# A tiny tanh in the first stage, and the last tile's convolution input ahead of its latents (two-layer decoder trunk, one core)

## The chip, the cores and the metric

The kernel runs on one core of a Trainium2 chip. The metric is device time of one execution in microseconds. Three runs of the kernel before took 896.16, 896.84 and 897.67 us; the median, 896.84 us, is the time before.

The core's engines work in parallel, each through its own instructions in a fixed order: TensorE (PE in the profile, with its weight loads as PEld), VectorE (DVE), ScalarE (ACT), GpSimd (POOL), and SyncE (SP), whose queue starts the DMAs. Semaphores hold an instruction until what it needs from another engine is done; all that stands behind it on its engine waits too.

## The reference

```python
D_MODEL, SEQ, DEPTH = 1024, 256, 2
for l in range(DEPTH):
    mod = c_act @ w_mod[l] + b_mod[l]                       # adaLN
    sh1, sc1, g1, sh2, sc2, g2 = jnp.split(mod, 6, axis=-1)
    h = modulate(rms_norm(x, mix_norm_g[l]), sh1, sc1)
    # token_mixer(h):
    z = h @ w_in
    q_lat, kv_lat, k_rope, qkv_b, conv_in, gate_logits = split(z)
    ...                                                     # o_a: MLA attention from q_lat, kv_lat, k_rope
    ...                                                     # o_b: MoBA attention from qkv_b
    glu_a, glu_g = jnp.split(conv_in, 2, axis=-1)
    u = glu_a * jax.nn.sigmoid(glu_g)
    u = causal_depthwise_conv(u, conv_dw_w, conv_dw_b)      # 31 taps
    o_c = silu(layer_norm(u)) @ w_conv_pw2 + b_conv_pw2
    y = (g[0] * o_a + g[1] * o_b + g[2] * o_c) @ w_out      # g: sigmoid gates
    x = x + g1 * y
    h = modulate(rms_norm(x, ffn_norm_g[l]), sh2, sc2)
    x = x + g2 * channel_mixer(h)                           # w_up, 3-tap conv, silu(a) * b, w_down
```

All inputs are fp32. x is 256 tokens by 1024 channels.

## The kernel before

Channels lie on the 128 partitions, tokens along the row, so x is 8 tiles (k = 0 to 7) of 128 x 256. Every fp32 product is made of three matmuls: each operand is split into a high part (`hi`, rounded by ACT's copy, L234) and a low part (`lo`, DVE's difference, L235), and PE adds hi*hi, hi*lo and lo*hi in one PSUM bank (L324, L325, L327). So each weight unit that SP loads (L206, tile `raw`) passes ACT (`whi`), then DVE (`wlo`), and then PE. `raw`, `whi` and `wlo` have four buffers each: a load waits until DVE has read the unit four before it, a split until PE is through with that unit's parts.

`all_units` lists the weight units in the order in which they are loaded and split; `take` hands them out in that order and keeps loads ahead (`AHEAD0`, two in the first stage). The program is written in one order, and the tile framework places each engine's instructions from it with priorities, so rows of different steps are interleaved. `issue_after` pins an instruction behind another.

The first stage of layer 0 is the loop `for k in range(KD)` in `layer`. For each tile k:

- ACT makes `e`, the modulated tile (L920), and from it `hh` (L921); DVE makes `hl` (L922). Both are operands for all of the layer's input projections.
- `latents(k)` adds the tile's part of q_lat, kv_lat and k_rope to three `psb` banks (weights 128x672), `conv_in(k)` that of the convolution input to four `psa` banks (128x1024).
- `prepare_tile(k + 1)` makes the next tile's modulation on DVE: one row of w_mod times c (1024 wide, L834) for tiles 0 to 3, two for 4 to 7, then `mod`, `mq` and `gs` (L836, L845, L841), on which the next `e` waits.
- After tile 2, ACT makes the sines for the rotary tables, with a function table of their own (L512).

Behind the loop the order of STEPS[0] begins: GLU0 to GLU3 (`glu`, L987 tanh on ACT, L988 product on DVE, which frees a psa bank each), LE0 and LE1 (`lat_evac`, the latents go from PSUM to SBUF on ACT, L955 to L958), LR0 (`lat_rstd`, three squares with sums on ACT, L967, `rs` on DVE, L544, and a power on POOL, L545), QKV00 (first of four units of the MoBA queries, into two psa banks), LR1, LT (`lat_T`: PE transposes the latents into psb banks, L975, two matmuls each, five pairs; ACT makes `qlh`/`klt` of them, L977, DVE `qll`/`klt`, L978), and QKV01 to QKV03. `kr` (L1136 to L1138) is the rotary key, which needs POOL's power. The 31 taps of the convolution (`cacc`, L1167 and L1170) are spread over the mixer on DVE. psa has five banks, of which the convolution input holds four; psb has three.

The tanh of the GLU and the sines are in different function tables, so ACT_TABLE_LOAD stands ahead of the first sine and, before the change, ahead of the first tanh of the GLU (L987).

Of the kernel before, what the change touches and what calls it, by code (L numbers as in the profile page):

```python
# [13 lines left out]
AF = mybir.ActivationFunctionType  # L14
# [7 lines left out]
KD = 8  # L22
# [36 lines left out]
LEAD = 16  # L59

LEADS = {(0, "G", 1, 0): 0, (0, "G", 1, 1): 40, (1, "G", 3, 0): 0, (1, "G", 3, 1): 40,
         (1, "in", 1): 0, (1, "in", 2): 40, (0, "up", 4, 0): 0, (0, "up", 4, 1): 40, (0, "up", 8, 0): 0, (0, "up", 8, 1): 40,
         (1, "up", 2, 1): 0, (1, "up", 3, 1): 40, (1, "up", 8, 0): 0, (1, "up", 8, 1): 40}
# [97 lines left out]
def trunk_kernel(ctx, tc, xT, crow, ccol, pos, invf, modb_d, cols_d, grow_d, wmh, wmr, wm, win1, wqkv,  # L161
                  wgc, wgab, wuq, wukv, woab, woc, wout, wup, wdn, out):
    nc = tc.nc
    te, ac, ve, gp, sy = nc.tensor, nc.scalar, nc.vector, nc.gpsimd, nc.sync
# [8 lines left out]
    def nm(s):  # L173
        uid[0] += 1
        return f"{s}_{uid[0]}"
# [4 lines left out]
    def psb():  # L180
        return psp.tile([P, 512], F32, tag="psb", name=nm("psb"), bufs=3)

    def e1():
        return wk.tile([P, S], F32, tag="e1", name=nm("e1"), bufs=8)
# [14 lines left out]
    def small(n, tag="sm", bufs=12):  # L199
        return wk.tile([P, n], F32, tag=tag, name=nm(tag), bufs=bufs)  # L200
# [37 lines left out]
    def chop(src, n, c, size=1024):  # L238

        m = max(1, size // c)  # L240
        return [(src[:, k0 * c:min(n, k0 + m) * c], range(k0, min(n, k0 + m))) for k0 in range(0, n, m)]

    def token_units(l, t):

        if t[0] == "KL":
            return [(win1[l, t[1], :, 0:672], [0])]
        if t[0] == "QKV":
            return [chop(wqkv[l, t[1], t[2] // 2], 4, 512)[t[2] % 2]]
        if t[0] in ("UQ", "UK"):
            return chop(wuq[l], 3, 768) if t[0] == "UQ" else chop(wukv[l], 2, 1024)  # L250
        if t[0] in ("C", "G"):
            return [chop((wgc if t[0] == "C" else wgab)[l, t[1]], KD, S)[t[2]]]
        if t[0] == "O":
            return chop(woab[l, t[1]], 1, 1024)
        if t[0] == "OC" and t[1] % 2 == 0:
            return chop(woc[l, t[1] // 2], 1, 1024)
        if t[0] == "PR" and t[1] % 2 == 0:
            return chop(wout[l, t[1] // 2], 2, 1024)
        return []

    def all_units():
        for l in range(L):
            for k in range(KD):
                if l == 0:
                    yield win1[l, k, :, 0:672], [0], LEAD
                yield win1[l, k, :, 672:1696], [0], LEADS.get((l, "in", k), LEAD)
            for t in CFG["order"][l]:
                yield from ((*u, LEADS.get((l, *t), LEAD)) for u in token_units(l, t))
            if l == 1:
                for first in (0, NRAW):  # L270
                    for i in range(2):
                        for j in range(first, first + NRAW):
                            yield *chop(wup[l, j], KD, S)[i], LEADS.get((l, "up", j, i), LEAD)
            for up, j in FFN[l]:
                if up and l == 1 and j < 2 * NRAW:
                    continue
                for i, u in enumerate(chop(wup[l, j], KD, S) if up else chop(wdn[l, j], 1, 1024)):
                    yield *u, LEADS.get((l, "up", j, i), LEAD) if up else LEAD

    ahead, later = [AHEAD0], [0]  # L280
    coming, raws_in, ready = list(all_units())[::-1], [], []

    def split_rest(keep=0):
# [16 lines left out]
    def take1():  # L300
        return take()[0][0][1]
# [10 lines left out]
    def flush(whole=False):  # L312
        if whole:

            banks = list(dict.fromkeys(id(o.tensor) for o, *_ in queue))
            queue.sort(key=lambda q: banks.index(id(q[0].tensor)))
            for o, p1, p2, p3, start, stop in queue:
                te.matmul(o, p1[0], p1[1], start=start, stop=False)
                te.matmul(o, p2[0], p2[1], start=False, stop=False)
                newest[0] = te.matmul(o, p3[0], p3[1], start=False, stop=stop)  # L320
            queue.clear()
            return newest[0]
        for o, p1, p2, _, start, _ in queue:
            te.matmul(o, p1[0], p1[1], start=start, stop=False)  # L324
            te.matmul(o, p2[0], p2[1], start=False, stop=False)  # L325
        for o, _, _, p3, _, stop in queue:
            last = te.matmul(o, p3[0], p3[1], start=False, stop=stop)  # L327
        queue.clear()
        return last

    def cut(w, i, n):
        return w[0][:, i * n:(i + 1) * n], w[1][:, i * n:(i + 1) * n]
# [23 lines left out]
    ones = cst.tile([P, 1], F32, name="ones")  # L356
# [62 lines left out]
    def mod_row(row, l, r, k, tag=None, scale=1.0):  # L419

        return use_row(wload_row(l, r, k, tag), row, l, r, k, scale)
# [57 lines left out]
    def step(gen, n=1):  # L479
        for _ in range(n):  # L480
            next(gen, None)
# [315 lines left out]
    def layer(l):  # L797
# [55 lines left out]
        def rows(pp, w, k, b, start, stop):  # L853
            mmv(pp, (hh[:, k, b * P:(b + 1) * P], hl[:, k, b * P:(b + 1) * P]), w, start, stop)

        def cols2(pp, w, k, first, last):
            for i in range(2):
                mmw(pp[:, i * S:(i + 1) * S], cut(w, i, P), (hh[:, k, :], hl[:, k, :]), first and i == 0,
                    last and i == 1)
# [15 lines left out]
        def gate_c(u, part, last=1, bank=psb):  # L875
            pp = pair(("C", u), part, bank)
            if part == last:
                if not gated:
                    gated.append(wk.tile([P, KD, S], F32, tag="thc", name=nm("thc"), bufs=1, align_bytes=LINE))
                ac.activation(gated[0][:, 2 * u:2 * u + 2, :].rearrange("p c t -> p (c t)"), pp, AF.Tanh, scale=0.5)  # L880
# [5 lines left out]
        def latents(k):  # L886
            if k == 0:
                plat.extend(psb() for _ in range(3))
            w = take1()
            st, sp = (k == 0), (k == KD - 1)  # L890
            for b in range(NB):
                rows(plat[b][:, 0:416], [v[:, 0:416] for v in w], k, b, st, sp)
                rows(plat[2][:, b * S:(b + 1) * S], [v[:, 416:672] for v in w], k, b, st and b == 0, sp and b == 1)
            flush()

        def conv_in(k):
            w = take1()
            for j in range(4):
                cols2(pci[j], cut(w, j, S), k, k == 0, k == KD - 1)
            flush()  # L900

        def tile(k):
            tiles.append(norm_tile(k, bc, gs1[:, k:k + 1], sh1[:, k:k + 1], hh, hl))
# [6 lines left out]
        for k in range(KD):  # L910
            if l > 0:
                if k + 3 < KD:
                    tile(k + 3)
                hold[0] = [i.ins for i in tiles[-1]]
                conv_in(k)
                hold[0] = None
                mod_row(crow1[0], l, 2, k, scale=0.5 if CDMA else 1.0)
                continue
            t = e1()
            ac.activation(t, xn[k // 4][:, k % 4, :], AF.Identity, scale=gains[k], bias=sh1[:, k:k + 1])  # L920
            at = ac.activation(hh[:, k, :], t, AF.Copy)  # L921
            last = ve.tensor_tensor(hl[:, k, :], t, hh[:, k, :].bitcast(F32), op=ALU.subtract)  # L922
            if HOLD > 1:
                hold[0] = [last.ins]
            with tc.issue_after(wlast[0].ins) if k == 0 else ExitStack():
                latents(k)
            if k == 2:
                with tc.issue_after(at.ins):
                    step(trigs)
            if k + 1 < KD:  # L930
                prepare_tile(k + 1)
            conv_in(k)
            if k in C0K:
                gate_c(0, C0K[k], 3, psa)
            hold[0] = None
# [576 lines left out]
    for l in range(L):  # L1512
        layer(l)
# [86 lines left out]
```

## Time and profile before

| | before |
|---|---|
| median of 3 runs | 896.84 us |
| profiled execution | 897.64 us |
| its span | 895.5 us |
| granted TensorE clock | 0.999 |
| DMA, mean over the span | 225 GB/s |
| first instruction of tile 6 on PE | 50.21 us |
| GLU's first tanh on ACT | 61.13 us |

The span runs from the first to the last instruction of the profiled execution; 2.14 us lie around it. In the timeline a row has start, duration, engine, line, operation, output<-inputs with shapes, a count where equal neighbours are merged, and in brackets the idle time just before it with what ended it. "By starts" means from the start of one instruction to the start of the next on its engine: since work is pipelined, that is a little shorter than its duration. Lines L are those of the kernel before; in the changed kernel they stand 1 lower in the file up to the stage's loop (L234 and L235 are unchanged) and 7 lower behind it.

### The profile page before, as it was taken

To read this page: it belongs to the slowest core of one execution; us is meant where nothing else is said; L and a number is where in the kernel's file an instruction comes from. 1 tells how busy PE (TensorE), PEld (TensorE's weight loads), DVE (VectorE), ACT (ScalarE), POOL (GpSimd) and SP (SyncE) were. 2 spreads that over 40 slices of the span, in tenths; PEclk is the share of its full clock that TensorE was granted. 3 is DMA by queue.
4 is the path that set the end of the run, shared out by engine and by line. 5 is a ranking of instruction groups with operands and counts; after the bars stand their busy time and mean duration, and the time that the engine had idled before them with its cause. 6 is when DMAs were issued, how large, how long until landed. Compare 5 with 4: busy or idle time off the path is not lost.

```text
span 895.5 us, 18568 instructions
## 1 busy us (share of the span) xinstructions
PE 876.3 (98%) x7233; PEld 833.4 (93%) x7233; DVE 806.8 (90%) x1592; ACT 555.6 (62%) x998; POOL 47.0 (5%) x36
## 2 busy tenths in 40 slices
PE   7899999999999999999999999999999999999998
PEld 6888888999998999999989988989999899999998
DVE  6989999999988989999956999999987899999774
ACT  4677588734756655455635676887575676646551
POOL 1000700000000000000000043000000000000000
PEclk9999999999999999999999999999999999999999
DMA  8956634689998788988725565156866475887631
GB/s 320 369 207 200 206 116 159 205 290 329 308 334 290 248 281 283 329 302 281 257 95 156 187 215 185 48 180 208 298 208 210 147 234 160 284 304 234 194 97 48
DMA packets 57975, 201.58 MB, mean 225 GB/s; under 512 B 6944, under 2 KB 8480, under 8 KB 57888
## 3 DMA queue, kind: packets, MB, share of 16 engines
q1 hardware_dynamic: 57888, 200.41, 67.0%
q8 instruction: 56, 0.92, 0.4%
q14 instruction: 31, 0.25, 0.1%
HBM read 199.33 MB, written 1.05 MB: 224 GB/s over the span
## 4 chain that ended last, share of the span: by engine, by line
PE 78%; DVE 12%; DMA 4%; ACT 4%; issue 2%; SPq 0%; DVEq 0%; ACTq 0%
PE psb L324 16%; PE psb L325 16%; PE psb L327 15%; PE psa L327 8%; PE psa L324 8%; PE psa L325 7%; DVE wlo L235 3%; DVE cacc L1170 2%; ACT whi L234 2%; DVE raw L834 1%; DMA raw<-in_wup 1%; PE psa L432 1%; PE psa L752 1%; PE psa L764 1%; DMA raw<-in_win 1%
## 5 line engine op out<-in xcount | busy, mean ns | idle before, releaser
L234 ACT ACTIVATE whi<-raw 128x1024 fp32r<-128x1024 f32 (+2 forms) x286 | 295.2, 1041 | 162.2 <-PE psb L325 79.1
L235 DVE TENSOR_TENSOR wlo<-raw,whi 128x1024 fp32r<-128x1024 f32 (+2 forms) x286 | 339.2, 1192 | 37.7 <-ACT whi L234 30.1
L324 PE MATMUL psb<-hh,whi 128*128 128x256 f32 x1056 | 254.6, 282 | 0.9 <-ACT hh L633 0.5
L325 PE MATMUL psb<-hl,whi 128*128 128x256 f32 x1056 | 252.3, 279 | 0.0
L324 PEld LDWEIGHTS psb<-hh,whi 128*128 128x128 f32 x1056 | 198.6, 188 | 5.5 <-issue 3.0
L325 PEld LDWEIGHTS psb<-hl,whi 128*128 128x128 f32 x1056 | 198.7, 188 | 0.1
L327 PE MATMUL psb<-hh,wlo 128*128 128x256 f32 x1056 | 144.5, 278 | 0.0
L327 PEld LDWEIGHTS psb<-hh,wlo 128*128 128x128 f32 x1056 | 131.3, 188 | 0.4 <-issue 0.3
L1170 DVE SCALAR_TENSOR_TENSOR cacc<-upad,cw,cacc 128x256 f32<-128x256 f32 x240 | 105.5, 475 | 0.5
L324 PE MATMUL psa<-mhl,whi 128*128 128x256 f32 x400 | 93.2, 276 | 0.0
L325 PE MATMUL psa<-mhl,whi 128*128 128x256 f32 x400 | 93.1, 277 | 0.0
L545 POOL TENSOR_TENSOR rs<-rs,mhalf 128x8 f32<-128x8 f32 (+3 forms) x26 | 45.5, 1763 | 671.7 <-DVE rs L544 671.6
L325 PEld LDWEIGHTS psa<-mhl,whi 128*128 128x128 f32 x400 | 74.9, 188 | 0.0
L324 PEld LDWEIGHTS psa<-mhl,whi 128*128 128x128 f32 x400 | 74.9, 188 | 0.0
L1468 DVE SCALAR_TENSOR_TENSOR e<-psb,fw,e 128x255 f32<-128x255 f32 (+1 forms) x168 | 69.7, 472 | 3.6 <-ACT e L1464 3.6
L415 DVE SCALAR_TENSOR_TENSOR raw<-raw,crow 128x1024 f32<-128x1024 f32 x56 | 67.9, 1214 | 0.0
L327 PE MATMUL psa<-mhl,wlo 128*128 128x256 f32 x400 | 53.5, 276 | 0.0
L327 PEld LDWEIGHTS psa<-mhl,wlo 128*128 128x128 f32 x400 | 49.1, 188 | 0.0
L1464 ACT ACTIVATE e<-psb,fb,fw 128x256 f32<-128x256 f32 x84 | 42.2, 553 | 4.4 <-PE psb L327 4.4
L1472 ACT ACTIVATE e<-e 128x256 f32<-128x256 f32 x44 | 18.2, 414 | 40.6 <-DVE e L1468 40.6
L1476 ACT ACTIVATE mhl<-e 128x256 fp32r<-128x256 f32 x44 | 18.2, 413 | 40.1 <-DVE e L1474 40.1
L324 PE MATMUL psb<-whi,hh 128*128 128x416 f32 (+1 forms) x96 | 31.0, 351 | 5.2 <-ACT hh L921 5.2
(295 smaller groups left out, 1525.5 us busy)
## 6 DMA issues: line engine op xcount, KB each, us to landing
raw<-in_wup SPq DMA_DIRECT2D x88, 512.0 KB, 5.2
raw<-in_wmr SPq DMA_DIRECT2D x68, 512.0 KB, 5.6
raw<-in_wdn SPq DMA_DIRECT2D x44, 512.0 KB, 4.5
raw<-in_wgab SPq DMA_DIRECT2D x32, 512.0 KB, 4.8
raw<-in_wqkv SPq DMA_DIRECT2D x24, 512.0 KB, 4.8
raw<-in_wm SPq DMA_DIRECT2D x24, 512.0 KB, 4.8
raw<-in_win SPq DMA_DIRECT2D x16, 512.0 KB, 5.3
raw<-in_wgc SPq DMA_DIRECT2D x16, 512.0 KB, 4.3
```

The source lines that it names most:

```text
L234: ac.activation(hi, raw, AF.Copy)
L235: ve.tensor_tensor(lo, raw, hi.bitcast(F32), op=ALU.subtract)
L324: te.matmul(o, p1[0], p1[1], start=start, stop=False)
L325: te.matmul(o, p2[0], p2[1], start=False, stop=False)
L327: last = te.matmul(o, p3[0], p3[1], start=False, stop=stop)
L415: ve.scalar_tensor_tensor(raw, raw, scale, row, op0=ALU.mult, op1=ALU.mult, accum_out=acc)
L545: gp.tensor_tensor(r, r, mhalf[:, :n], op=ALU.pow)
L1170: ve.scalar_tensor_tensor(aj, upad[:, j, t:t + S], cw[:, j * 31 + t:j * 31 + t + 1], aj, op0=ALU.mult, op1=ALU.add)
L1464: ac.activation(t, src, AF.Identity, scale=fw[:, 2, c:c + 1], bias=fb[:, c:c + 1])
L1468: ve.scalar_tensor_tensor(t[:, d:S], src[:, 0:S - d], fw[:, 2 - d, c:c + 1], t[:, d:S], op0=ALU.mult, op1=ALU.add)
L1472: ac.activation(th, ab[0], AF.Tanh, scale=0.5)
L1476: ac.activation(mh, th, AF.Copy)
```

## The change

```diff
     def all_units():
         for l in range(L):
             for k in range(KD):
+                two = [(win1[l, k, :, 672:1696], [0], LEADS.get((l, "in", k), LEAD))]
                 if l == 0:
-                    yield win1[l, k, :, 0:672], [0], LEAD
-                yield win1[l, k, :, 672:1696], [0], LEADS.get((l, "in", k), LEAD)
+                    two.insert(0 if k < KD - 1 else 1, (win1[l, k, :, 0:672], [0], LEAD))
+                yield from two
...
             with tc.issue_after(wlast[0].ins) if k == 0 else ExitStack():
-                latents(k)
+                if k < KD - 1:
+                    latents(k)
             if k == 2:
                 with tc.issue_after(at.ins):
                     step(trigs)
+            if k == 4:
+                with tc.issue_after(at.ins):
+                    ac.activation(small(1, "m0", 4), ones, AF.Tanh)
             if k + 1 < KD:
                 prepare_tile(k + 1)
             conv_in(k)
+            if k == KD - 1:
+                latents(k)
```

In layer 0, a tanh of one column is placed behind `hh` of tile 4, and its table load with it. In tile 7 the 1024-wide unit of the convolution input is loaded, split and used ahead of the 672-wide unit of the latents. The instructions of the two kernels are otherwise the same; their order changes in more places, since the framework places them anew.

**ACT at the end of the first stage.** Before, from `hh` of tile 6 (`whi_674` is tile 7's 672-wide unit, `whi_703` its 1024-wide one, `whi_737` that of QKV00):

```order
L234 ACTIVATE whi_674<-raw_672 128x672
L921 ACTIVATE hh_135<-e_110_668 128x256
L234 ACTIVATE whi_703<-raw_701 128x1024
L920 ACTIVATE e_121_731<-mq_257,mod_100,gs_698 128x256
L921 ACTIVATE hh_135<-e_121_731 128x256
L234 ACTIVATE whi_737<-raw_735 128x1024
L234 ACTIVATE whi_755<-raw_753 128x1024
L955 ACTIVATE ma_831<-psb_293 128x384
```

Now (`whi_676` is tile 7's 1024-wide unit, `whi_705` its 672-wide one, `whi_739` QKV00, `whi_769` QKV01, `whi_855` QKV02):

```order
L922 ACTIVATE hh_135<-e_111_670 128x256
L234 ACTIVATE whi_676<-raw_674 128x1024
L234 ACTIVATE whi_705<-raw_703 128x672
L921 ACTIVATE e_122_733<-mq_257,mod_100,gs_700 128x256
L234 ACTIVATE whi_739<-raw_737 128x1024
L922 ACTIVATE hh_135<-e_122_733 128x256
L234 ACTIVATE whi_769<-raw_767 128x1024
L234 ACTIVATE whi_855<-raw_853 128x1024
L994 ACTIVATE e_143_821<-psa_285 128x256
```

QKV00's split moved between `e` and `hh` of tile 7, QKV02's split moved ahead of the GLU, and the GLU's tanh (L994) ahead of the latents' evacuation, with no table load before it.

**PE between tiles 6 and 7**, now (before, tile 7's latents stood here directly behind tile 6):

```order
L328 MATMUL psa_288<-hh_135,wlo_643 128x256 x2
L325 MATMUL psa_851<-whi_739,hh_135 128x512
L326 MATMUL psa_851<-whi_739,hl_136 128x512
L325 MATMUL psa_285<-hh_135,whi_676 128x256
L325 MATMUL psa_286<-hh_135,whi_676 128x256
```

The first two matmuls of QKV00 (`psa_851`, the fifth bank) moved ahead of all of tile 7.

**DVE behind the GLU's products.** Before (`wlo_854` and `wlo_860` are QKV02 and QKV03, `rs_846` the sums of the first 128 tokens, `kr_834` their rotary key, `qll` the latents' low parts):

```order
L235 TENSOR_TENSOR wlo_854<-raw_851,whi_853 128x1024
L544 TENSOR_SCALAR rs_846<-lss_841 128x3
L235 TENSOR_TENSOR wlo_860<-raw_857,whi_859 128x1024
L978 SCALAR_TENSOR_TENSOR qll_810<-psb_883,col_146,qlh_809 128x256
L978 SCALAR_TENSOR_TENSOR qll_810<-psb_888,col_146,qlh_809 128x256
L544 TENSOR_SCALAR rs_880<-lss_875 128x3
L1136 TENSOR_SCALAR kr_834<-kr_834,rs_846 128x32
```

Now:

```order
L235 TENSOR_TENSOR wlo_862<-raw_859,whi_861 128x1024
L545 TENSOR_SCALAR rs_848<-lss_843 128x3
L1177 SCALAR_TENSOR_TENSOR cacc_1299<-upad_814,cw_803,cacc_1299 128x256
L1143 TENSOR_SCALAR kr_836<-kr_836,rs_848 128x32
L985 SCALAR_TENSOR_TENSOR qll_812<-psb_885,col_146,qlh_811 128x256
L545 TENSOR_SCALAR rs_882<-lss_877 128x3
L1144 TENSOR_TENSOR kr_836<-kr_836,ta_793 128x32
L985 SCALAR_TENSOR_TENSOR qll_812<-psb_890,col_146,qlh_811 128x256
```

`kr`, which waits for POOL's power of `rs_848`, moved ahead of the first `qll`, and a tap stands between `rs_848` and it.

**PE at the fourth pair of transposes.** Before, they stood inside QKV01 (`whi_755`); now they follow its last matmul:

```order
L328 MATMUL psa_852<-wlo_770,hh_135 128x512
L982 MATMUL psb_900<-ident,ma_833 128x128
L982 MATMUL psb_900<-ident,ma_838 128x128
L325 MATMUL psa_851<-whi_855,hh_135 128x512
L982 MATMUL psb_905<-ident,ma_833 128x128
```

`psb_900` takes the bank of the first pair, so it waits until `qll` of `psb_885` has read that, and `psb_905` until `qll` of `psb_890` has. On SP the two loads of tile 7's input weights trade places (the 1024-wide one now comes first); on POOL nothing moves.

## The prediction

> **What bounds the kernel now.** I read the page's busy shares first, then the stretches, then TensorE's waits behind the first stage, and last the timeline between 38 and 70 us, engine by engine.
>
> ```profile
> PE 876.3 (98%) x7233; PEld 833.4 (93%) x7233; DVE 806.8 (90%) x1592; ACT 555.6 (62%) x998; POOL 47.0 (5%) x36
> ...
> 40.00:62.00 22.00, 19.63 (x144) 18.36 (x142) 19.39 (x48) 13.44 (x26) 0.00 (x0) 1.00 0.75 281
> 62.00:112.00 50.00, 49.84 (x249) 42.13 (x249) 49.69 (x106) 35.02 (x59) 19.22 (x9) 1.00 0.59 191
> ...
> PE psa L324 <- DVE upad L988: 1.1, 1, 1.1
> PE psb L568 <- DVE mod L416: 0.5, 1, 0.5
> PE psb L324 <- DVE b L1230: 0.3, 1, 0.3
> ```
>
> The stretches give TensorE (PE), weight loads, VectorE (DVE), ScalarE (ACT), GpSimd (POOL) in this order. From 62 us on, PE and DVE are both full (49.84 and 49.69 of 50); only the first stage has room, 2.4 us of 22 on PE. The three waits are all that PE has between 62 and 223 us. The first is the stall that this change aims at. So a gain is at most what PE waits near 50 to 62 us plus 0.8 later, and a loss must come from a new wait of PE or from DVE falling back, since DVE has no gaps to catch up in.
>
> ```profile
> 50.21 0.77 PE L324 MATMUL psb<-whi,hh 128*128 128x416 f32 x3 [0.56 <-ACT hh L921]
> ...
> 54.04 1.07 PE L327 MATMUL psa<-hh,wlo 128*128 128x256 f32 x8
> 55.11 0.76 PE L324 MATMUL psb<-whi,hh 128*128 128x416 f32 x3
> 56.44 0.77 PE L325 MATMUL psb<-whi,hl 128*128 128x416 f32 x3 [0.21 <-DVE hl L922]
> ...
> 60.52 0.40 PE L325 MATMUL psa<-whi,hl 128*128 128x512 f32 x1
> 62.02 0.51 PE L324 MATMUL psa<-whi,hh 128*128 128x512 f32 x1 [1.10 <-DVE upad L988]
> ...
> 64.44 0.82 PE L975 MATMUL psb<-ident,ma 128*128 128x128 f32 x6
> ...
> 68.31 0.39 PE L324 MATMUL psa<-whi,hh 128*128 128x512 f32 x1
> ```
>
> Tile 6 starts at 50.21, tile 7's latents at 55.11. The first two matmuls of QKV00 go into the fifth psa bank; the next needs a bank that the GLU has read, and comes at 62.02. By starts, 512-wide matmuls follow each other every 0.23 us, 256-wide ones every 0.12. The marks I compare are 64.44 (QKV00 done) and 68.31 (QKV01 and ten transposes done, QKV02 begins).
>
> **The table load.**
>
> ```profile
> 38.93 0.40 ACT L921 ACTIVATE hh<-e 128x256 fp32r<-128x256 f32 x1
> 40.55 1.07 ACT L234 ACTIVATE whi<-raw 128x1024 fp32r<-128x1024 f32 x1 [1.22 <-DMA raw<-in_win]
> ...
> 43.06 1.22 DVE L235 TENSOR_TENSOR wlo<-raw,whi 128x1024 fp32r<-128x1024 f32 x1
> ...
> 57.67 0.49 ACT L955 ACTIVATE ma<-psb 128x384 f32<-128x384 f32 x1 [0.71 <-PE psb L327]
> ...
> 59.17 0.56 ACT L967 ACTIVATE b<-ma 128x384 f32<-128x384 f32 x1
> 59.58 0.23 ACT L967 ACTIVATION_READ_ACCUMULATOR b<-ma 128x1 f32 x1
> 59.83 1.28 ACT L987 ACT_TABLE_LOAD   x1
> 61.13 1.21 ACT L987 ACTIVATE e<-psa 128x256 f32<-128x256 f32 x4
> ...
> L789 ACT ACTIVATE sm<-cc 128x8 f32<-128x8 f32 x1 | 0.2, 208 | 0.4 <-DMA cc<-in_ccol 0.4
> ```
>
> The load of 1.28 us stands between the latents' evacuation and the four tanh of the GLU, on PE's path. Now it stands behind hh of tile 4: 39.33 + 1.28, and 0.2 for the tiny tanh (the 128x8 one takes 208 ns), ends near 40.85. ACT idled there until 40.55 for a transfer, so the split behind it slips 0.3 and ends by 41.9. DVE takes it up at 43.06, after tile 5's modulation rows. Cost: nothing. The cover is that wait for the transfer; without it the 1.5 us would still have 43.06 less 41.62, or 1.4, before DVE is touched. The tiny tanh reads a constant and issues no DMA.
>
> [...]
>
> **Tile 7's convolution input first.** What it moves on ACT and DVE costs more than the swap suggests.
>
> ```profile
> 48.59 0.60 ACT L920 ACTIVATE e<-mq,mod,gs 128x256 f32<-128x256 f32 x1 [2.40 <-DVE gs L841]
> 49.10 0.75 ACT L234 ACTIVATE whi<-raw 128x672 fp32r<-128x672 f32 x1
> 49.76 0.40 ACT L921 ACTIVATE hh<-e 128x256 fp32r<-128x256 f32 x1
> ...
> 54.00 0.60 ACT L920 ACTIVATE e<-mq,mod,gs 128x256 f32<-128x256 f32 x1 [2.89 <-DVE gs L841]
> 54.64 0.42 ACT L921 ACTIVATE hh<-e 128x256 fp32r<-128x256 f32 x1
> 54.96 2.00 ACT L234 ACTIVATE whi<-raw 128x1024 fp32r<-128x1024 f32 x2
> ...
> 49.88 0.86 DVE L235 TENSOR_TENSOR wlo<-raw,whi 128x672 fp32r<-128x672 f32 x1 [0.19 <-ACT whi L234]
> 50.66 0.42 DVE L922 TENSOR_TENSOR hl<-e,hh 128x256 fp32r<-128x256 f32 x1
> 51.00 1.22 DVE L834 SCALAR_TENSOR_TENSOR raw<-raw,crow 128x1024 f32<-128x1024 f32 x1
> ```
>
> - Tile 6: hh comes straight behind e (48.59 + 0.64 = 49.23), ahead of a split, so PE starts at 49.70, 0.5 sooner, and ends near 54.5 (54.04 + 1.07 less 0.5).
> - Split of tile 7: DVE does hl (49.69 to 50.03), then waits for the 1024-wide whi (49.55 + 1.06 = 50.61) and works 1.14 to the next start. The modulation rows begin at 51.78, not 51.00: **0.78 late**. So e of tile 7 starts at 54.78, not 54.00.
> - ACT now has QKV00's split (0.94 by starts: two in 2.00 at 54.96) between e and hh: 55.29 to 56.35, hh at 56.65. PE's row has QKV00's first matmul next, which needs that split: PE stands from 54.5 to 56.40, **1.9 us**, where it stood 0.2 and 0.4 by starts (55.11 and 56.44). Queued behind on PE are all of tile 7 and, through it, the GLU.
> - Then no wait: QKV00 x2 0.46, convolution x4 0.47, latents x3 0.60, QKV00 0.23 (58.16); hl has arrived (DVE: narrow split from 54.67, tables, QKV00's split from 56.40, hl 57.54 to 57.96); convolution x20 2.3 (60.44), latents 1.46 (61.90), three of QKV00 (62.59).
> - GLU: ACT's split for QKV02 waits for the last use of that buffer at 59.7 and ends 60.8; tanh from 60.69. DVE does that split's lower half from 60.84, the GLU from 61.98; the bank is free at 62.45, before 62.59. **The stall of 1.27 us (60.75 to 62.02 by starts) is gone**; six more matmuls end QKV00 at 63.97.
>
> Sum so far: removed 0.5 + 0.2 + 0.4 + 1.27 = 2.4, added 1.9, mark 1 at 63.97 for 64.44: **0.47 gained**. Of the DMAs, the last tile's two weight loads trade sizes in their queue places; the larger, issued near 39.9, has 9 us until it is used, so nothing.
>
> **What is late next.** The latents now end last, their evacuation and squares come 1.5 us of ACT time later, and the rows of DVE put kr behind a POOL result and ahead of the first qll, which frees the psb bank of the fourth transpose pair.
>
> ```profile
> 64.93 1.22 DVE L235 TENSOR_TENSOR wlo<-raw,whi 128x1024 fp32r<-128x1024 f32 x1
> 66.06 0.93 DVE L978 SCALAR_TENSOR_TENSOR qll<-psb,col,qlh 128x256 fp32r<-128x256 f32 x2
> 67.81 0.96 DVE L235 TENSOR_TENSOR wlo<-raw,whi 128x768 fp32r<-128x768 f32 x1
> ...
> 65.10 1.76 POOL L545 TENSOR_TENSOR rs<-rs,mhalf 128x3 f32<-128x3 f32 x1 [53.59 <-DVE rs L544]
> 67.14 0.85 POOL L545 TENSOR_TENSOR rs<-rs,mhalf 128x3 f32<-128x3 f32 x1 [0.28 <-DVE rs L544]
> ...
> L1170 DVE SCALAR_TENSOR_TENSOR cacc<-upad,cw,cacc 128x256 f32<-128x256 f32 x240 | 105.5, 475 | 0.5
> ```
>
> ACT: evacuation from 61.81 (1.50, as 57.67 to 59.17), squares and one split until 65.99. DVE: the next split (65.2 at its whi's end, taken from 64.92), rs at 66.06, a tap (475 ns) until 66.62. POOL's work took 0.85 alone, and 1.76 when a DVE split ran until 66.15: then it ended 0.71 later. Behind the tap I take 66.62 + 0.70 = 67.32; bounds 67.00 (no wait) and 68.06 (1.76). Then kr 67.43, qll 67.58 to 68.06. PE, with six transposes (0.57) and QKV01 (2.76) behind 63.97, is there at 67.30 and **waits 0.8**, then 0.1 for the second qll. Mark 2: 68.71 for 68.31, so **0.40 lost** (0.1 to 1.1 by the bounds). Queued behind kr on DVE stand the qll and the next splits: the split that started at 67.81 starts at 69.35, but three taps and one kr (1.35) are already done: DVE is 0.2 behind.
>
> [...]
>
> **Behind 70 us.**
>
> ```profile
> 181.31 1.15 DVE raw L415 x2
> ...
> 220.92 0.33 DVE e L561
> ```
>
> Some orders shift up to about 210 us, with the same work. PE is 0.4 late, DVE 0.2, and the chain of waits runs mostly through DVE between these two pieces, 181 to 221 us, where the waits of 0.5 and 0.3 leave PE a little room. I take the middle: **+0.3**. The profiled execution took 897.64 (span 895.5 and 2.14 around it), so 897.9; the median 896.84 becomes **897.1**.
>
> **Rivals.**
> - *Faster: POOL's result comes in time.* Then mark 2 is 67.30 and two pairs (0.48), 67.78, 0.5 early, and if order shifts also remove the later 0.8, 1.3: 895.5 to 896.3, I say 896.1. For it: rs waits on ACT times that I stacked to 0.1 us over 15 steps. Against: even at 67.00 PE would wait.
> - *Slower: both POOL calls meet a long DVE operation* and take 1.76, as at 65.10. PE loses 1.1 at mark 2, DVE 0.2 + 0.75 + 0.9 = 1.85, and where DVE is the chain (181 to 222) that sets the end: 898.7. It decides once DVE's lag exceeds PE's 1.1. Against: DVE's row has short operations there.
> [...]
>
> **How the numbers follow.** Forecast 0.50, faster rival 0.25, slower rival 0.20, drain 0.05. The range runs from the faster rival's 895.5 to the slower one's 898.7, and 0.2 outward at both ends for the spread of the runs (896.16 to 897.67): 895.3 to 898.9. Under 0.2% (1.8 us, about what a measurement of this kernel can tell from no change) is "same". Faster takes 0.07 of the faster rival and 0.04 of the forecast's edge: 0.11. Slower takes 0.12 of the slower rival and 0.05 of the edge: 0.17. Same: 0.72.
>
> **What would show it.** In the changed profile: a table load near 39.3 us without later idle; no wait for upad at L995; a PE gap of near 1.9 us before the first QKV matmul, ended by whi; a PE wait of near 0.8 on qll at the fourth transpose pair, with DVE idle before kr until POOL ends. No such wait, or POOL done before 66.9, breaks the forecast downward; POOL calls over 1.5 us break it upward; a new PE wait over 1 us between 100 and 220 us would be something I have not seen.

## The result, and the profile after

The changed kernel takes **901.6 us** (median of 14 runs, 898.84 to 908.71) against 896.81 for the kernel before (median of 14, 895.76 to 901.51). The ratio is 1.0057, with a 95% interval of 1.0036 to 1.0078: slower by about half a per cent, and outside the range that was forecast. The profiled execution took 903.09 us, with a span of 901.0.

The engines' busy times on the page, first, say that busy time grew on PE, a little on POOL, and hardly on any other engine:

```profile
PE 880.3 (98%) x7233; PEld 836.6 (93%) x7233; DVE 807.0 (90%) x1592; ACT 555.3 (62%) x999; POOL 48.7 (5%) x36
```

PE has 4.0 us more than before for the same 7233 matmuls, POOL 1.7, DVE practically the same. So part of the 5.5 us of span is in matmuls that take longer. The prediction's two stretches and the one behind them show where (columns: length, then busy time of PE, weight loads, DVE, ACT, POOL, then TensorE's granted clock, DMA share, GB/s), and behind them four pieces of 3.41 us. Before, the third stretch was this:

```profile
112.00:162.00 50.00, 49.85 (x427) 42.83 (x427) 48.55 (x107) 44.16 (x121) 1.73 (x2) 1.00 0.45 149
```

And in the changed kernel:

```profile
40.00:62.00 22.00, 19.64 (x135) 18.79 (x135) 18.72 (x46) 10.86 (x18) 0.00 (x0) 0.92 0.78 277
62.00:112.00 50.00, 47.66 (x235) 39.97 (x234) 47.27 (x102) 35.87 (x65) 19.07 (x8) 1.00 0.56 178
112.00:162.00 50.00, 49.82 (x405) 42.26 (x403) 46.51 (x100) 39.45 (x105) 3.56 (x3) 0.97 0.40 135
...
53.84:57.25 3.41, 1.61 (x10) 1.42 (x10) 3.41 (x12) 2.81 (x4) 0.00 (x0) 1.00 0.49 154
57.25:60.66 3.41, 3.41 (x16) 3.28 (x16) 1.94 (x10) 0.19 (x1) 0.00 (x0) 0.50 0.74 196
108.46:111.87 3.41, 1.79 (x12) 1.66 (x13) 3.41 (x8) 2.63 (x5) 3.41 (x2) 1.00 0.46 157
111.87:115.28 3.41, 3.41 (x13) 2.59 (x12) 2.22 (x5) 0.00 (x0) 3.41 (x3) 0.50 0.50 150
```

Two things are new. Between 62 and 112 us PE has 2.3 us of room, where it had 0.2. And the clock column, 1.00 in all three stretches before, is 0.92 in the first and 0.97 in the third. The four short pieces resolve that: the clock is not a little lower for long but half for 3.41 us, twice, and each time straight behind a piece in which PE stood idle for half of it (1.61 and 1.79 us busy of 3.41). Half speed for 3.41 us is, by that arithmetic, 1.7 us of matmuls lost; I call such a piece a dip.

TensorE's waits between 40 and 230 us name the idle pieces:

```profile
PE psa L696 <- ACT qkT L1159: 2.0, 1, 2.0
PE psa L325 <- ACT whi L234: 1.8, 1, 1.8
PE psb L325 <- ACT hh L922: 0.5, 1, 0.5
PE psb L982 <- DVE qll L985: 0.4, 1, 0.4
```

The second and the fourth were forecast (1.9 and 0.8), the wait for upad is gone as forecast. The first, 2.0 us for the first scores of the latent attention, is the new wait "over 1 us between 100 and 220 us" that the prediction called unseen. PE's timeline, from tile 6 to those scores:

```profile
52.87 1.07 PE L328 MATMUL psa<-hh,wlo 128*128 128x256 f32 x8
55.74 0.50 PE L325 MATMUL psa<-whi,hh 128*128 128x512 f32 x1 [1.80 <-ACT whi L234]
...
60.23 1.32 PE L328 MATMUL psa<-hh,wlo 128*128 128x256 f32 x8
...
64.83 0.82 PE L982 MATMUL psb<-ident,ma 128*128 128x128 f32 x6
...
68.77 0.44 PE L982 MATMUL psb<-ident,ma 128*128 128x128 f32 x2 [0.35 <-DVE qll L985]
...
110.08 1.16 PE L696 MATMUL psa<-qkT 96*128 96x128 f32 x8 [1.99 <-ACT qkT L1159]
```

Compare the eight 256-wide matmuls at 52.87 and at 60.23: the same work, 1.07 us at full clock, 1.32 where the first 0.4 us of it fall into the slow piece.

What the scores waited for is read backwards through ACT, DVE and POOL (each engine's timeline, ACT first):

```profile
106.97 1.06 ACT L1059 ACTIVATE mq<-mq 128x1024 f32<-128x1024 f32 x1 [3.18 <-DVE ss L1061]
107.93 1.04 ACT L234 ACTIVATE whi<-raw 128x1024 fp32r<-128x1024 f32 x1
108.88 0.57 ACT L1159 ACTIVATE qkT<-psa 96x512 f32<-96x512 f32 x1
...
101.10 0.69 DVE L1129 TENSOR_TENSOR ma<-ma,rs 128x512 f32<-128x512 f32 x1 [1.23 <-POOL rs L546]
102.70 0.69 DVE L1141 TENSOR_TENSOR ma<-kv,rs 128x512 f32<-128x512 f32 x1 [0.57 <-POOL rs L546]
...
94.77 6.29 POOL L546 TENSOR_TENSOR rs<-rs,mhalf 128x16 f32<-128x16 f32 x1 [0.32 <-DVE rs L545]
```

qkT comes behind a square on ACT that waited 3.18 us for DVE's reduction; DVE had stood 1.23 and 0.57 us for two GpSimd powers; and the first of these, 128x16, took 6.29 us. Before, the same call took 3.34, and DVE did not wait:

```profile
93.95 3.34 POOL L545 TENSOR_TENSOR rs<-rs,mhalf 128x16 f32<-128x16 f32 x1
```

### The profile page after: what moved, and what is told of

Read it like the earlier page. It is cut to its first block, busy times and chain, and to the rows that moved or that the text cites. A ratio compares the mean times of both kernels' runs of the same rounds, so it can differ in the third digit from the quotient of the medians.

```text
span 901.0 us, 18572 instructions
## 1 busy us (share of the span) xinstructions
PE 880.3 (98%) x7233; PEld 836.6 (93%) x7233; DVE 807.0 (90%) x1592; ACT 555.3 (62%) x999; POOL 48.7 (5%) x36
## 4 chain that ended last, share of the span: by engine, by line
PE 78%; DVE 12%; ACT 5%; DMA 4%; issue 1%; SPq 0%; POOL 0%; DVEq 0%; ACTq 0%
PE psb L325 16%; PE psb L326 16%; PE psb L328 15%; PE psa L328 8%; PE psa L326 7%; PE psa L325 7%; DVE wlo L235 3%; DVE cacc L1177 3%; ACT whi L234 2%; PE psa L433 1%; ACT p L732 1%; DVE raw L835 1%; PE psa L753 1%; PE psa L319 1%; DMA raw<-in_wmh 1%
```

## The experiments

Theory A puts the loss on the swap of tile 7, not on the moved table load; theories C (the clock) and E (GpSimd) say how the swap does it. Their rivals are B (the load), D (the dips are incidental) and F (ACT's moved rows cause the wait for qkT). Ratios are to the kernel before, in runs on the same chip, with 95% intervals.

### Each part alone

The tiny tanh alone (first e1, and once more as e10) leaves every row of PE, DVE, POOL and ACT in its place, but for the load and the tiny tanh:

```diff
+            if k == 4:
+                with tc.issue_after(at.ins):
+                    ac.activation(small(1, "m0", 4), ones, AF.Tanh)
             if k + 1 < KD:
                 prepare_tile(k + 1)
             conv_in(k)
```

> Only the tiny tanh, tile 7 as before. Theory A (the loss comes from what tile 7's swap does to the order of work and to TensorE's gaps): the table load leaves the GLU's path, the 1.27 us stall before QKV00's second pair goes, no new gap comes: 895.5 us, ratio 0.9985, granted clock 0.998 or more in the profile. Rival B (the moved table load costs something by itself, for example by draining ScalarE at tile 4): 897.5 us or more, with DVE or PE late between 40 and 50 us.

> The tiny tanh alone once more, to see whether it is faster than the kernel before: theory A has 1.3 us less than before, ratio 0.9985; no TensorE wait over 0.6 us between 55 and 600 us. If the ratio is 0.9995 or more, the stall of the GLU was not worth its length.

Measured: 895.62 us, ratio 0.9991 (0.9976 to 1.0007), and in the second run 895.2 us, **0.9983 (0.9974 to 0.9992)**. The moved load is a gain, of 0.8 us by the first run, whose interval includes no change, and 1.5 us by the second. The second run's ACT and PE show it:

```profile
38.63 1.28 ACT L932 ACT_TABLE_LOAD   x1
39.92 0.20 ACT L932 ACTIVATE m<-ones 128x1 f32<-128x1 f32 x1
40.52 1.06 ACT L234 ACTIVATE whi<-raw 128x1024 fp32r<-128x1024 f32 x1 [0.40 <-DMA raw<-in_win]
...
59.10 1.21 ACT L990 ACTIVATE e<-psa 128x256 f32<-128x256 f32 x4
...
49.50 0.76 PE L324 MATMUL psb<-whi,hh 128*128 128x416 f32 x3 [0.56 <-ACT hh L921]
...
60.05 0.45 PE L324 MATMUL psa<-whi,hh 128*128 128x512 f32 x1
...
62.40 0.82 PE L978 MATMUL psb<-ident,ma 128*128 128x128 f32 x6
```

Behind the load ACT still waits 0.40 us for its transfer, so the load is hidden whole. From tile 6's start to the first transposes PE needs 12.90 us (49.50 to 62.40), before 14.23 (50.21 to 64.44): 1.33 gained, the stall of 1.27 us of the prediction. Rival B falls.

The swap alone (the tiny tanh taken out again, tile 7 as in the changed kernel):

> Only the swap of tile 7, the table load stays in front of the GLU. Theory A: the two bad places of the changed kernel are here as well (TensorE waits 1.8 us for whi ahead of QKV00 and near 2 us for qkT at about 108 us, with clock dips behind them), and the load is on the path again: 901 to 903 us, ratio 1.005 to 1.007. Rival B: without the moved load the loss is gone: 896 to 897.5 us.

Measured: 901.45 us, 1.0045 (1.0031 to 1.0059). The loss is all here. TensorE's waits are 1.85 us for whi and 3.02 for qkT. The dips came otherwise than expected: in the profiled execution none behind the first gap, and behind the second one of double length, 6.83 us from 110.62. So the same gap ahead of QKV00 does not bring a dip in every execution.

```profile
112.30 2.07 PE L696 MATMUL psa<-qkT 96*128 96x128 f32 x8 [3.02 <-ACT qkT L1156]
```

### Is it the clock?

A filler of 14 matmuls on a constant was to stand in the gap ahead of QKV00.

```diff
                 pqkv[i] = [psa() if i < 2 else psb() for _ in range(2)]
+                if l == 0 and i == 0:
+                    warm(pqkv[i][0], 14)
```

> The changed kernel with 14 matmuls on a constant (about 1.6 us) put into TensorE's gap ahead of QKV00; no row of another engine moves. Theory C (the gap costs 1.7 us more than its own length, because the granted clock halves for 3.4 us behind it): no clock under 0.99 between 55 and 62 us, QKV00 done near 63.1 instead of 64.8, time 0.5 to 1.7 us under the changed kernel's 901.6, so 900 to 901; the wait for qkT near 108 us stays. Rival D (the dip is incidental and the new wait near 108 us is the whole loss): time unchanged at 901.6 us, or the dip is still there.

Measured: 901.41 us, 1.0050 (1.0032 to 1.0068), with dips at 56.9 and 111.5 us. This was a miss of the edit: nothing held the filler, and it ran at 15.12 us, in an idle piece of the first tiles. It serves as a control: the filler in another place helps nothing. In the next run it was held behind tile 6's last matmul, and later with half the number.

```diff
+            if k == KD - 2:
+                tile6.append(newest[0].ins)
...
                 if l == 0 and i == 0:
+                    with tc.issue_after(tile6[0]):
+                        warm(pqkv[i][0], 14)
```

> The changed kernel; 14 matmuls on a constant (1.6 us) now held behind tile 6's last matmul, so that they stand in TensorE's gap ahead of QKV00; no row of another engine moves. Theory C (a gap of 1.8 us halves the granted clock for 3.4 us behind it and so costs 1.7 us more than its length): no clock under 0.99 between 55 and 62 us, tile 6's start to the first transposes takes 14.1 us instead of 15.8. As the wait for qll behind it may grow to 1.2 us, only 0.3 to 1.7 us of it arrive at QKV02, and the time is 900 to 901.3 us; the wait for qkT near 108 us stays. Rival D (the dip does not come from the gap): a dip within 55 to 62 us all the same, 15.8 us, 901.5 us.

> The pinned filler with 7 matmuls instead of 14, so that about 1.0 us of TensorE's gap ahead of QKV00 is left in one piece. Theory C with a threshold (idle time of 1.5 us within a window of 3.4 us was left without a dip in the traces so far, 1.6 us was not): no dip between 55 and 62 us, time as with the full filler, ratio 1.003. Rival (any gap near 1 us brings the dip): a dip at 57 us and the ratio of the changed kernel, 1.005 or more.

Measured: 14 matmuls 899.27 us, **1.0031 (1.0017 to 1.0046)**, faster than the range expected; 7 matmuls 898.75 us, **1.0032 (1.0019 to 1.0044)**. The changed kernel as it is, beside the latter on the same chip:

> The changed kernel as it is, beside the others on the same chip. Theories C and E: ratio 1.0045 to 1.006; the mean granted clock over its runs 0.003 to 0.004 under that of the kernel before, which is about two more dips of 3.4 us in 900 in each run. Rival D (the dips are incidental): the same mean clock as the kernel before.

Measured: 902.17 us, 1.0066 (1.0053 to 1.0079). So work that computes nothing, put into an idle piece, saves 3.4 us on that chip, and some 2 to 3 us if the ratio with 14 is set beside the changed kernel's two ratios, 1.0057 and 1.0066. No row of another engine moved. PE's timeline with 14, and the stretch from 55 to 62 us in it:

```profile
54.39 1.70 PE L349 MATMUL psa<-warm_w 128*128 128x256 bf16 x14
56.38 0.51 PE L325 MATMUL psa<-whi,hh 128*128 128x512 f32 x1 [0.28 <-ACT whi L234]
...
63.96 0.82 PE L985 MATMUL psb<-ident,ma 128*128 128x128 f32 x6
...
55.00:62.00 7.00, 6.72 (x51) 6.19 (x49) 5.99 (x20) 4.84 (x10) 0.00 (x0) 1.00 0.65 192
```

QKV00 starts no sooner (it waits for the same whi), but from there to the transposes it takes 7.58 us instead of 9.09 (55.74 to 64.83): 1.5 less, with the clock at 1.00. The half filler left a gap of 1.07 us in one piece, and took 7.57: a gap of that length did no harm there. The saving is larger than the 1.7 us of one dip, and the mean clock says why. A dip lowers the mean over 900 us by 3.41 x 0.5 / 900 = 0.0019. The changed kernel's five runs have a mean of 0.9936, the kernel before 0.9978 beside it: 2.2 dips more. With 7 fillers it is 0.9972, 0.3 more. With 14 it is 0.9955 beside 0.9974: on average one dip more was left over the twelve runs, though the profiled execution shows none in the program. The two gaps lie 54.3 us apart (55.74 and 110.08), the dips 54.6 = 16 x 3.41, so that both gaps fall on nearly the same place of the 3.41 us grid: in both profiles of the changed kernel, and in that of the loose filler, both bring a dip. Once the first brings none, all that follows comes 1.5 us sooner and the second gap falls elsewhere on the grid; neither profile with a pinned filler has a second dip. That the place on the grid is the reason is argued from this and not tried by itself. Rival D, that the dips are incidental, falls.

### Is it GpSimd?

One power of layer 0 is left out (128x16, batch 1), then this and its neighbour (128x8). The rows of PE, DVE and ACT stay in their order.

```diff
-            qrr = rstd_of(qss, 16, 1.0 / 64.0)
+            qrr = rstd_of(qss, 16, 1.0 / 64.0, skip=l == 0 and b == 1)
```

> The changed kernel without one GpSimd power of layer 0 (128x16, batch 1, of the query norms of the latent attention), so its result is not used as a norm; every row of PE, DVE and ACT stands where it stood. Theory E (the new wait for qkT comes from DVE waiting 1.8 us for two GpSimd calls, of which the first takes 6.3 us there instead of 3.3): DVE's waits of 1.2 and 0.6 us near 101 us go or fall under 0.5 us together, ACT's wait for ss shrinks by as much, PE's wait of 2.0 us for qkT near 108 us falls under 0.4 us and the clock dip behind it goes: 2.0 + 1.7 less, 897.5 to 899 us. Rival F (the moved rows of ACT cause the wait, GpSimd only happens to be late): PE still waits 1.5 us or more near 108 us, 901 us.

Measured: 898.19 us, 1.0026 (1.0013 to 1.0039), but the wait for qkT was still there, 1.74 us. By its time this run meets theory E, by its wait rival F: in that the expectation failed. The profile tells why:

```profile
94.28 7.43 POOL L547 TENSOR_TENSOR rs<-rs,mhalf 128x8 f32<-128x8 f32 x1 [0.53 <-DVE rs L545]
...
109.13 1.16 PE L697 MATMUL psa<-qkT 96*128 96x128 f32 x8 [1.74 <-ACT qkT L1160]
```

Now the 128x8 call, which takes 1.63 us elsewhere, took 7.43 in the same place, and DVE waited 1.53 us for it. So it is not the size of a call alone that counts, but where it stands. The two stretches of this profile with the gaps in them show another thing:

```profile
55.00:62.00 7.00, 5.55 (x40) 5.37 (x41) 5.98 (x19) 4.84 (x10) 0.00 (x0) 1.00 0.62 185
105.00:120.00 15.00, 13.25 (x96) 11.32 (x95) 15.00 (x30) 11.03 (x30) 7.34 (x4) 1.00 0.40 135
```

Both gaps were there (1.82 and 1.74 us), and the clock stayed at 1.00: the same gaps bring a dip in one execution and not in another. Over the twelve runs the mean clock is 0.9964 beside 0.9974, half a dip more than before, where the changed kernel had 2.2. So, as far as the mean clock shows it, most of what this run saves is in dips that did not come, and not in the wait.

> The changed kernel without both GpSimd powers of batch 1's norms in the latent attention (128x16 and 128x8), so that no GpSimd call is left between 94 and 105 us; rows of PE, DVE and ACT as in the changed kernel, TensorE's gap ahead of QKV00 left in. With only one of them left out, the other took 7.4 us and the wait for qkT was still 1.74 us. Theory E (GpSimd calls that cannot end while DVE runs without pause are what delays the scores): no wait of DVE between 94 and 105 us, PE's wait for qkT near 108 us under 0.4 us in the profile, time 898 us (897.3 to 898.8: the gap ahead of QKV00 and its dip remain). Rival F (the moved rows of ACT): PE still waits 1.5 us for qkT.

Measured: 897.46 us, **1.0014 (1.0005 to 1.0023)**. DVE's waits for POOL are gone, and PE's wait is

```profile
PE psa L697 <- ACT qkT L1160: 0.2, 1, 0.2
```

with ACT's rows in the changed kernel's order; ACT's square waits 1.41 us for DVE's reduction instead of 3.18. Rival F falls. The gap ahead of QKV00 is there, 1.80 us, but the dip expected behind it did not come in the profiled execution. From the first scores to the first 512-wide matmul behind them PE needs 8.61 us here (107.40 to 116.01) and 10.30 in the changed kernel (110.08 to 120.38): 1.69, one dip.

Both edits in one, and the control for the left-out call:

> Both edits in one: the pinned filler ahead of QKV00 and the left-out GpSimd power. Theories C and E together: no dip behind 30 us, no TensorE wait over 1 us between 60 and 200 us, 896.5 to 898 us, that is within 0.2% of the kernel before. If the sum is over 899.5 us, something else of the loss has not been found.

> Control: the tiny tanh alone, without the same GpSimd power. There the call took 3.3 us and nothing waited for it. Theory E: no change against the tiny tanh alone, 895 to 896.3 us. If it falls by 1 us or more, leaving out the call is worth something by itself, and the run without it in the changed kernel is to be read less that.

Measured: filler and left-out power 896.05 us, **1.0001 (0.9992 to 1.0010)**: nothing of the loss against the kernel before is left. In this profile the wait for qkT is gone as well, although only the 128x16 call is left out, as in the first of these runs: the 128x8 call took 5.05 us instead of 7.43, and DVE did not wait for it.

```profile
93.75 5.05 POOL L548 TENSOR_TENSOR rs<-rs,mhalf 128x8 f32<-128x8 f32 x1 [0.40 <-DVE rs L546]
```

The rows of DVE and ACT have the same order in both profiles, so their order alone does not set the length of such a call; what else does is open. The control took 894.2 us, below the range expected: 0.9975 (0.9965 to 0.9986), against 0.9983 (0.9974 to 0.9992) and 0.9991 (0.9976 to 1.0007) with the call, on other chips. The intervals overlap, but up to 0.7 or 1.4 us of the gain of each run that leaves the call out may be the call itself. The wait for qkT, which goes from 1.99 to 0.22 us without both calls, does not hang on this.

### A swap without the gap

Here the weight splits of tile 7's convolution step are held behind tile 7's hh, all else as changed.

```diff
+            if k == KD - 1:
+                hold[0] = [at.ins]
             conv_in(k)
             if k == KD - 1:
                 latents(k)
```

> The changed kernel with the weight splits of tile 7's convolution step held behind tile 7's hh, so that ScalarE makes hh first. The gap of 1.8 us ahead of QKV00 should fall under 0.7 us in all theories. Theory C: no dip near 57 us, QKV00 done near 63. If the order of rows near 90 to 108 us then lets the POOL results come in time, 895.5 to 897 us; if the wait for qkT of 2 us stays, 899 to 900 us. Rival D: 901 us if that wait stays, whatever the clock does at 57 us.

Measured: 896.12 us, 0.9987 (0.9972 to 1.0002). The gap is 1.30 us, not under 0.7: ACT is free at once, but PE has nothing else to do until hh. No dip followed it in the profiled execution. Around 94 us DVE's rows came out as in the kernel before, and so did GpSimd's call:

```profile
92.95 3.35 POOL L546 TENSOR_TENSOR rs<-rs,mhalf 128x16 f32<-128x16 f32 x1 [1.16 <-DVE rs L545]
```

PE waits 0.2 us for qkT. That fits E with no work left out, but ACT's square and qkT also stand in their old order here, so this run alone would not tell E from F. This kernel and the tiny tanh alone (0.9983 and 0.9991) are the fastest that keep all the work, and the intervals do not separate them.

## Why the prediction was wrong

Measured from tile 5's start, since whole executions shift by half a microsecond (44.80 before, 44.15 after, 44.65 with both powers left out):

| point | before | forecast | after | after's order, no dip (e9) |
|---|---|---|---|---|
| tile 6 starts (50.21 before, 49.05 after) | 5.41 | 4.90 | 4.90 | |
| QKV00 done, mark 1 | 19.64 | 19.17 | 20.68 | 19.15 |
| wait for whi ahead of QKV00 | 0 | 1.9 | 1.80 | 1.80 |
| wait for qll at the fourth pair | 0 | 0.8 | 0.35 | 0.46 |

- **The table load: right.** ACT's rows of the changed kernel show it hidden in the same place as e10's do:

```profile
38.70 1.28 ACT L934 ACT_TABLE_LOAD   x1
39.99 0.20 ACT L934 ACTIVATE m<-ones 128x1 f32<-128x1 f32 x1
40.56 1.07 ACT L234 ACTIVATE whi<-raw 128x1024 fp32r<-128x1024 f32 x1 [0.36 <-DMA raw<-in_win]
...
54.14 0.60 ACT L921 ACTIVATE e<-mq,mod,gs 128x256 f32<-128x256 f32 x1 [3.53 <-DVE gs L842]
54.64 1.04 ACT L234 ACTIVATE whi<-raw 128x1024 fp32r<-128x1024 f32 x1
55.59 0.40 ACT L922 ACTIVATE hh<-e 128x256 fp32r<-128x256 f32 x1
```

  The load ends 0.01 us ahead of the tiny tanh and starts 0.02 behind hh; in the kernel before 0.02 us lay on either side of it (59.83). The split behind comes at 40.56, no later than before (40.55). The drain, idle time of ACT around a load, to which the prediction gives a chance of 0.05, shows in no run: these gaps of 0.01 and 0.02 us are what stands in its place.
- **Tile 7: right in order and size, wrong in price.** Tile 6 gained 0.5, the split came between e (54.14) and hh (55.59), PE stood 1.80 us for the 1.9 forecast. But the gap was counted at its own length, and every matmul behind it at full clock, since no row of before showed anything but 1.00. In this execution the clock was 0.50 for 3.41 us behind it: 1.5 us more at mark 1. This is the first term that failed: PE's time behind the gap. In e9, with the same order and the same gap but no dip, mark 1 comes 19.15 us behind tile 5, against 19.17 forecast.
- **The GLU's stall: right.** Gone in the changed kernel and in e10, worth 1.33 us there.
- **What is late next: right, a little large.** POOL's call took 1.02 us and ended at 68.04, 0.71 behind the end of the tap (67.33), where the forecast had taken 0.70 from the one call at 65.10. The call of 0.85 us before, which the prediction calls alone, ran beside a qll on DVE (67.12 to 67.60). kr came behind POOL's call, PE waited 0.35 to 0.46 us for qll instead of 0.8.
- **Behind 70 us: the step that failed most.** "With the same work" was true, and "I take the middle: +0.3" was not: the rows of DVE near 94 us had changed places (the product of L1131, for one, stood ahead of a weight split that it had stood behind), a GpSimd call took 6.29 us for 3.34, and through DVE and ACT PE waited 2.0 us at 108. Behind that came a second dip, 1.7 us. The order of these rows was known before the run, and the prediction did not ask what it might do to the calls, although the step at 65 us had weighed just that. The lengths could not have been read off the order: with the same order of DVE's rows the 128x16 call took 6.29 us here and 7.83 in the swap alone.
- **The rivals.** The slower one named GpSimd calls that meet long DVE operations, at 66 us. That came nearest, at another place: it reckoned 1.06 us more for a call (1.76 instead of 0.70), and the call near 94 us took 2.95 more than before. No rival had the clock.

The sum for the profiled execution: mark 2 comes 1.2 us later than forecast (one matmul of QKV02 now stands ahead of the last transposes and the second starts at 69.52, which counts as 69.29, 25.14 behind tile 5's start, forecast 23.91; the smaller wait for qll gave 0.3 of the 1.5 back), then 2.0 for qkT and 1.7 behind it: 4.9. The forecast of 897.9 for that execution and 4.9 give 902.8; it took 903.09. That this is so near is partly luck: this execution was 0.65 us ahead at tile 5's start, which leaves 902.2, and the rest is mostly one more wait, which is not in the sum:

```profile
240.31 0.39 PE L325 MATMUL psb<-uh,whi 128*128 128x256 f32 x1 [1.10 <-ACT uh L1215]
```

In the second profile of the changed kernel (901.13 us) it is 0.23 us. Its cause was not tried.

## What to carry to other kernels

An idle piece of TensorE near 2 us had two prices here: its length (1.80 and 1.99 us), and in some executions nearly the same again (1.5 and 1.7 us) behind it at half clock. Where a change opens such a gap on TensorE's path, add it to the sum or fill the gap with matmuls that compute nothing, as the kernel with 7 fillers did, which took 3.4 us less than the changed kernel on the same chip. And where a change moves rows around GpSimd calls that others wait for, follow those calls through the new order, however far from the edit: here more than half of the loss came 50 us later than the swap.

## What was not expected of the hardware

**The granted clock.** In the changed kernel's profile the granted clock falls to 0.50 at 19.71, 57.26 and 111.87 us, for 3.41 us each, behind gaps of 1.82, 1.80 and 1.99 us. The starts lie 37.55 and 54.61 us apart, 11.0 and 16.0 times 3.413 us, so they lie on one grid; in its second profile (19.40, 56.95 and 111.56) they lie the same distances apart. That one grid runs through a whole execution is assumed here. I placed the grid in each of the fourteen profiles by its dips, the one at the program's end included, and took PE's idle time in each window behind 15 us: of 23 windows with 1.55 to 2.01 us idle, 12 were followed by a dip, of 29 with 0.9 to 1.5 us, one (1.29 us, at 706.95 us without both powers). Idle time alone does not decide it. These two windows of the kernel with 7 fillers had 1.57 us idle around the scores, and no dip followed, where the changed kernel's 108.46 row, with 1.62, brought one:

```profile
108.19:111.60 3.41, 1.84 (x12) 1.71 (x13) 3.41 (x8) 2.57 (x5) 3.41 (x2) 1.00 0.48 163
111.60:115.01 3.41, 3.41 (x25) 2.92 (x24) 3.41 (x8) 1.29 (x3) 3.41 (x3) 1.00 0.41 144
```

No dip followed the gaps at 18 and 25 us of the kernel before (1.80 and 2.29 us in its profile); in the control without the power (e8) one came at 26.59 us, behind a window with 2.00 us idle. The changed kernel's dip at 19.71 left tile 5's start at 44.15 us, no later than the 44.80 of before: the wait of 2.29 us for hh, at 25.36 us before, is not there in the changed kernel and may have taken it up.

**GpSimd's calls.** One 128x8 power took 1.6 to 2.7 us, or 5.05 and 7.43, one 128x16 power 2.9 to 3.9, or 6.29 and 7.83 us. The calls of 6.29, 7.43 and 7.83 us ended 1.2, 1.5 and 2.8 us after DVE had run out of work, as theory E has it. But before, a call of 3.34 us (93.95 to 97.29) ended while DVE went from one operation with two inputs to the next without a pause, and with the filler and one power left out the call of 5.05 us ended at 98.80 us, while DVE worked on until past 105 us. Why these ended while DVE worked and the three did not was not tried and stays open.
